# First mixer of a two-block transformer kernel: gate blocks between the heads, two softmaxes combined before the division, and GpSimd's wide steps given to other engines

## The chip, the cores and the metric

One core of a Trainium2 chip runs the whole program. The time is that of one execution on the device, in microseconds (us), as the median of three runs. Five engines work their own instruction lists in order and wait for each other by semaphores: TensorE (PE, matrix products), VectorE (DVE), ScalarE (ACT), GpSimd (POOL) and SyncE (SP, which here starts the weight transfers).

## The reference, cut to what matters

256 tokens of width 1024 pass through a feed-forward block, a mixer, a second feed-forward block, and then a second block of another kind, which the change doesn't touch. The mixer of the first block is:

```python
h = rmsnorm(x, g_pre_mix[l])
z = h @ w_in[l]
qa, ka, va, qd, kd, vd, ga, gb = jnp.split(z, cuts, axis=-1)
...
oa = diff_attention(qa, ka, va, lam)                 # 8 heads, two softmaxes each
oa = (rmsnorm(oa, g_subln[l]) * (1.0 - lambda_init)).reshape(B, S, DA_V_W)
...                                                  # 12 dilated heads in 3 groups: qd, kd, vd
od = jnp.sum(wts[..., None].astype(x.dtype) * jnp.stack(outs, axis=0), axis=0)
merged = jax.nn.sigmoid(ga) * (oa @ w_proj_a[l]) + jax.nn.sigmoid(gb) * (od @ w_proj_b[l])
x = x + rmsnorm(merged @ w_out[l], g_post_mix[l])
```

and inside `diff_attention`:

```python
s = jnp.einsum('bqhcd,bkhcd->bhcqk', qblk, k, preferred_element_type=jnp.float32) * scale
p = jax.nn.softmax(s, axis=-1)
a = p[:, :, 0] - lam * p[:, :, 1]
return jnp.einsum('bhqk,bkhe->bqhe', a.astype(v.dtype), v, ...)
```

## The kernel before, in words

All weights come as one stream of blocks of 128x1024 (512 KB), in the order in which `_stream` lists them. For each block ACT casts the raw weights to a rounded part wh (L243), and another engine subtracts it to get the rest, wl (L245): DVE, or POOL for every second block while `ws.pool_every` is 2. A product with such a block is three matmuls for each of its eight slices: wh with hT, wh with lT, wl with hT (L297 to L299), 24 matmuls for a column block of q, k or a gate. A block is split some blocks ahead of its use: each call of `ws.next()` puts one more cast and one more subtraction into the lists of ACT and DVE, at the place of the call.

The order of every engine's list is the order of the code. The work on attention is written as generators, which a pump holds; each `pump.step()` takes each active generator to its next `yield`, between two blocks of PE's products.

The first mixer runs in these stages. V of the heads (va). Then a loop over eight heads, two weight blocks each: q block, step, k block, step. A head (`diff_head`) takes several steps while the next heads' blocks are computed: rope (a shuffle on DVE, a product with ropeC on POOL, one with ropeS and a sum on DVE, giving qr), scores (PE into two banks acc), `exps` (a maximum and a scaled negative nb on DVE for each of the two score tiles, then two exponentials on ACT with row sums ls), the combination of the two softmaxes (ACT scales one by nb, DVE adds the other), four transposes (tr), a copy (aT), the product with va, and a copy of it into ov.

Then come the six dilated pairs of (s, g) in `MIX_ORDER`, two weight blocks each. After the third one, six blocks of V (vz) and the first gate blocks follow, and the other gate blocks after the sixth. Each dilated pair has its rope, its scores with a mask, its exponentials into the tile ed; after the third of a set, eight rounds of transposes, copies (eT) and products (od), then weights from the maxima (`weights`), a weighted sum over the groups (part), two transposes and a split (odH, odL). `subln` squares ov, sums it by head, takes the power -0.5 on POOL, multiplies ov, and transposes it into oaH and oaL. A list named `lock` sets which of the two sets and `subln` uses the transposes' banks. Last are the projection of oa (eight blocks), the merge with that of od, and w_out.

PSUM has eight banks here: two of tag mm (the blocks), three acc (scores), one od, two tr (transposes, products with va).

Of the kernel before, what the change touches and what calls it, by code (L numbers as in the profile page):

```python
# [50 lines left out]
# ---------------------------------------------------------------- layout on the host  # L51
# [22 lines left out]
GATES_A = 2  # L74
# [3 lines left out]
def _stream(a):  # L78
# [4 lines left out]
    qb, kb = _col_blocks(qa, 8, 1), _col_blocks(ka, 8, 1)  # L83
    for h in range(8):
# [3 lines left out]
    gab, gbb = _col_blocks(ga, 8, 1), _col_blocks(gb, 8, 1)  # L88
    gates = [w for c in range(8) for w in (gab[c], gbb[c])]
# [129 lines left out]
# ---------------------------------------------------------------- on the chip  # L219
# [57 lines left out]
def body(ctx, tc, a, o, upto=99):  # L277
# [17 lines left out]
    # matmul helpers on split operands  # L295
# [11 lines left out]
    def gemm_pair(outs, xs, shared=False):  # L307
        """Two products of the same operand, a block of it at a time; shared: outs lie in one bank."""
# [13 lines left out]
    def keep_busy(n, pt):  # L322
        """Keeps the tensor engine's clock up while it waits."""
# [15 lines left out]
    # ---- constants  # L339
# [31 lines left out]
    def inv_root(r, s, eps):  # L371
        """r = (s + eps) ** -0.5"""
# [4 lines left out]
    def row_sum(pool, src, p=128):  # L377
        """Mean squares of the rows."""
# [5 lines left out]
    def finish(acc, ops):  # L384
        """The last two steps of a token-major gemm, the first tile of tokens ahead of the second."""
# [5 lines left out]
    class RowNorm:  # L391
        """r = (mean square over factor ** 2 + eps over factor ** 2) ** -0.5 of 128 rows, by halves of the columns."""
# [17 lines left out]
    def close(pool, acc, g, factor, gi, tags, early=lambda n: None, fills=(), rest=20):  # L410
        """x += factor * rmsnorm(acc) * g, or x += acc, or x; hT, lT = the split of (rmsnorm(x) * g_pre) transposed."""
# [71 lines left out]
    def norm_meta(pool, gi):  # L483
        """hT, lT of the meta tokens."""
# [17 lines left out]
    # ---- feed-forward  # L502
# [47 lines left out]
    # ---- hyena filter in time; two thirds of its last product wait for turns of the tensor engine  # L550
# [55 lines left out]
    def mixer_tables(FP):  # L606
# [17 lines left out]
        # -lambda on all partitions  # L624
# [24 lines left out]
    # ---- mixer of the first block  # L649
    with tc.tile_pool(name="mix", bufs=1) as MP:  # L650
# [19 lines left out]
        def qk_block(qk, i):  # L670
            pt = psum("mm")
            gemm_w(pt[:, :T], ws.next(), xs_x)
            nc.scalar.copy(qk[:, i, :], pt[:, :T])
# [4 lines left out]
        def rope_pair(qk, res):  # L678
# [3 lines left out]
            nc.gpsimd.tensor_tensor(qk, qk, ropeC[:, None, :].to_broadcast([128, 2, T]), op=ALU.mult)  # L682
# [909 lines left out]
```

## Time and profile before

| | us |
|---|---|
| median of three runs | 1844.4 |
| lowest, highest of them | 1843.55, 1852.92 |
| span of the profiled execution (its own time lies around it) | 1849.8 |
| first mixer: V of the heads | from 209 to 232 |
| its loop over heads | from 232 to 345 |
| its dilated pairs, gates and projection | from 345 to 458 |
| its merge and w_out | from 458 to 495 |

The span counts from the first to the last instruction. PE's busy share of it is 95%, and the granted clock of PE over the whole span is 0.987 of full speed. An instruction that is busy on an engine off the path costs nothing by itself; what ends last is told by the chain of waits, and where PE stands by its timeline, in which a bracket tells how long it was idle before an instruction and which instruction released it.

### The profile page before, as it was taken

The page shows a single profiled execution, that of the slowest core. Times are in us where ns is not written, and L with a number is a line of the kernel's source. Part 1 is how long each engine was busy: PE and PEld are TensorE (multiplying, and loading weights), DVE is VectorE, ACT ScalarE, POOL GpSimd, SP SyncE. Part 2 cuts the span into 40 slices and gives each one's busy share as a digit, 9 for nine tenths or more (in the row PEclk, how much of TensorE's full clock was granted, in tenths as well). Part 3 has the DMA queues.
Part 4 walks back from the last instruction along what each step waited for, and adds up shares of the span by engine and source line. Part 5 has one row for each costly group of instructions (what it writes and reads, how often), then busy time and mean ns, then how long its engine had stood idle before and what let it go on. Part 6 is the DMA issues. An engine that isn't in the chain of part 4 may idle for free.

```text
span 1849.8 us, 30894 instructions
## 1 busy us (share of the span) xinstructions
PE 1750.3 (95%) x11794; PEld 1592.4 (86%) x11794; DVE 1343.0 (73%) x2040; ACT 927.6 (50%) x1495; POOL 725.8 (39%) x609
## 2 busy tenths in 40 slices
PE   8999998999999998899799899998999999999998
PEld 7999888999899977878789899998888888888886
DVE  5665678664655648985868998788888867777776
ACT  5544555554564435555445344454544445544554
POOL 3000133312200206444413354799999933322332
PEclk9999999999999999999999999999999999999999
DMA  7555543444565533433365457655555567767775
GB/s 237 190 176 186 162 145 104 149 129 160 183 205 196 180 135 120 146 105 100 115 193 185 146 196 234 206 178 176 178 176 163 170 233 256 244 227 234 250 242 173
DMA packets 93412, 332.09 MB, mean 180 GB/s; under 512 B 10552, under 2 KB 10707, under 8 KB 90960
## 3 DMA queue, kind: packets, MB, share of 16 engines
q1 hardware_dynamic: 79488, 287.73, 47.8%
q0 software_dynamic: 3696, 21.67, 3.4%
q10 hardware_dynamic: 10080, 20.71, 3.1%
q8 instruction: 93, 1.52, 0.3%
q14 instruction: 55, 0.45, 0.1%
HBM read 311.73 MB, written 18.35 MB: 178 GB/s over the span
## 4 chain that ended last, share of the span: by engine, by line
PE 59%; DVE 18%; POOL 12%; ACT 4%; issue 4%; DMA 3%; ACTq 0%; POOLq 0%; SPq 0%; DVEq 0%
PE mm L297 9%; PE mm L299 9%; PE mm L298 9%; POOL oh L1477 8%; PE acc L299 7%; PE acc L298 7%; PE acc L297 7%; DVE wl L245 5%; POOL wl L245 3%; PE od L297 2%; PE od L298 2%; PE od L299 2%; ACT wh L243 2%; DVE xc L1069 1%; DVE hu L1248 1%
## 5 line engine op out<-in xcount | busy, mean ns | idle before, releaser
L245 DVE TENSOR_TENSOR wl<-raw,wh 128x1024 fp32r<-128x1024 f32 x462 | 634.9, 1379 | 272.3 <-ACT wh L243 271.7
L297 PE MATMUL mm<-hT,wh 128*128 128x256 f32 (+1 forms) x2496 | 721.0, 289 | 8.0 <-DVE th L1281 4.7
L299 PE MATMUL mm<-hT,wl 128*128 128x256 f32 (+1 forms) x2496 | 709.0, 284 | 11.0 <-DVE wl L245 11.0
L298 PE MATMUL mm<-lT,wh 128*128 128x256 f32 (+1 forms) x2496 | 710.8, 285 | 0.0
L243 ACT CAST wh<-raw 128x1024 fp32r<-128x1024 f32 x544 | 568.3, 1049 | 271.4 <-PE mm L298 64.8
L297 PEld LDWEIGHTS mm<-hT,wh 128*128 128x128 f32 x2496 | 477.0, 191 | 18.1 <-issue 5.5
L299 PEld LDWEIGHTS mm<-hT,wl 128*128 128x128 f32 x2496 | 479.4, 192 | 12.2 <-DVE wl L245 12.2
L298 PEld LDWEIGHTS mm<-lT,wh 128*128 128x128 f32 x2496 | 477.2, 191 | 3.5 <-issue 1.4
L245 POOL TENSOR_TENSOR wl<-raw,wh 128x1024 fp32r<-128x1024 f32 x82 | 204.0, 2488 | 233.0 <-ACT wh L243 186.7
L1477 POOL TENSOR_SCALAR oh<-iota,eT 128x128 fp32r<-128x128 f32 x256 | 233.8, 930 | 11.3 <-PE acc L1488 11.3
L299 PE MATMUL acc<-wh,al 128*128 128x512 f32 x516 | 202.1, 392 | 0.7 <-DVE al L337 0.7
L298 PE MATMUL acc<-wl,ah 128*128 128x512 f32 x516 | 202.0, 391 | 0.5 <-DVE wl L245 0.4
L297 PE MATMUL acc<-wh,ah 128*128 128x512 f32 x516 | 202.1, 392 | 0.0
L1478 DVE SCALAR_TENSOR_TENSOR oh<-iota,eT,wp 128x256 fp32r<-128x256 f32 x256 | 147.4, 610 | 0.1
L403 POOL TENSOR_SCALAR ssq<-ssq 128x1 f32<-128x1 f32 x18 | 8.5, 471 | 299.0 <-ACT junk L401 270.0
L299 PEld LDWEIGHTS acc<-wh,al 128*128 128x128 f32 x516 | 96.9, 188 | 22.9 <-DVE al L337 1.7
L298 PEld LDWEIGHTS acc<-wl,ah 128*128 128x128 f32 x516 | 96.8, 188 | 20.9 <-DVE wl L245 1.6
L297 PEld LDWEIGHTS acc<-wh,ah 128*128 128x128 f32 x516 | 96.9, 188 | 19.3 <-issue 0.3
L336 ACT CAST ah<-sv 128x256 fp32r<-128x256 f32 x124 | 50.2, 405 | 111.4 <-PE od L298 43.0
L1520 POOL TENSOR_TENSOR sv<-sv,gd 128x512 f32<-128x512 f32 x62 | 96.1, 1580 | 6.1 <-DMA sv<-act 5.8
L337 DVE TENSOR_TENSOR al<-sv,ah 128x256 fp32r<-128x256 f32 x124 | 72.3, 583 | 33.4 <-ACT ah L336 33.4
L1512 POOL DMA_DIRECT2D sv<-act x16 | 9.6, 599 | 213.2 <-DVE al L337 209.2
(388 smaller groups left out, 2334.9 us busy)
## 6 DMA issues: line engine op xcount, KB each, us to landing
raw<-in_ws_dram SPq DMA_DIRECT2D x288, 512.0 KB, 3.7
raw<-in_us_dram SPq DMA_DIRECT2D x128, 512.0 KB, 3.7
raw<-in_vs_dram SPq DMA_DIRECT2D x128, 512.0 KB, 4.3
act<-st ACTq DMA_DIRECT2D x62, 256.0 KB, 3.0
sv<-act POOLq DMA_DIRECT2D x15, 1024.0 KB, 7.8
gate_w<-in_gate_w_dram ACTq DMA_DIRECT2D x2, 1024.0 KB, 7.0
gain<-in_gains_dram POOLq DMA_DIRECT2D x3, 512.0 KB, 6.4
res<-x SPq DMA_DIRECT2D x2, 512.0 KB, 4.5
```

Source lines behind the costliest of these rows:

```text
L243: nc.scalar.copy(h, raw)
L245: eng.tensor_tensor(lo, raw, h.bitcast(F32), op=ALU.subtract)
L297: nc.tensor.matmul(out, lh, rh, start=start, stop=False)
L298: nc.tensor.matmul(out, lh, rl, start=False, stop=False)
L299: nc.tensor.matmul(out, ll, rh, start=False, stop=stop)
L336: nc.scalar.copy(h, src)
L337: (eng or nc.vector).tensor_tensor(lo, src, h.bitcast(F32), op=ALU.subtract)
L1069: nc.vector.scalar_tensor_tensor(out, src, w, out, op0=ALU.mult, op1=ALU.add)
L1248: nc.vector.scalar_tensor_tensor(out, t[:, j:j + L], w, out, op0=ALU.mult, op1=ALU.add)
L1477: nc.gpsimd.tensor_scalar(o1, iota, eT[tt][:, 0, tl:tl + 1], None, op0=ALU.is_equal)
L1478: nc.vector.scalar_tensor_tensor(oh, iota[:, None, :].to_broadcast([128, 2, 128]), eT[tt][:, 1, tl:tl + 1], wp[:, :, tl:tl + 1].bitcast(F3 ...
L1520: nc.gpsimd.tensor_tensor(src, src, gd[:, e:e + 2, :], op=ALU.mult)
```

## The change

It concerns the first mixer alone. The stream of weights now has a gate block behind each head's q and k, and the other eight gate blocks together behind the dilated pairs. The scale of the scores goes into ACT's copy of q, so the maxima need no product: `exps` takes a maximum with its sign turned. The two softmaxes of a head are combined as e0 + r1 * e1 with r1 = -lam * l0 / l1, and the division by l0 is left to ACT, as the scale of the copy of the product with va. POOL's product with ropeC goes to DVE, behind the shuffle, with a `yield` less. POOL's weight subtractions go to DVE (`pool_every` stays 0). `subln` is added after the first dilated pair instead of the third, squares on ACT and multiplies on DVE, and has its transposes before the first set's od; the sums of part and of the merge go from POOL to DVE. The two small operations of the power -0.5 stay on POOL. Comments go, by which line numbers shift.

```diff
     for h in range(8):
-        units += [qb[h], kb[h]]
+        units += [qb[h], kb[h], gab[h]]
...
         if n == 2:
-            units += list(vb) + gates[:2 * GATES_A]
-    units += gates[2 * GATES_A:]
+            units += list(vb)
+    units += list(gbb)
...
+            if i:
+                nc.scalar.copy(qk[:, i, :], pt[:, :T])
+            else:
+                nc.scalar.activation(qk[:, i, :], pt[:, :T], AF.Copy, scale=DA_SCALE)
...
             nc.vector.stream_shuffle(sw, qk, SWAP)
-            nc.gpsimd.tensor_tensor(qk, qk, ropeC[:, None, :].to_broadcast([128, 2, T]), op=ALU.mult)
-            yield
+            nc.vector.tensor_tensor(qk, qk, ropeC[:, None, :].to_broadcast([128, 2, T]), op=ALU.mult)
...
-                nc.vector.tensor_reduce(mx[:, :, c], sc[c], axis=AX.X, op=ALU.max)
-                nc.vector.tensor_scalar(nb[:, :, c], mx[:, :, c], -DA_SCALE, None, op0=ALU.mult)
+                nc.vector.tensor_reduce(nm[:, :, c], sc[c], axis=AX.X, op=ALU.max, negate=True)
...
-            nc.vector.reciprocal(ls, ls)
-            nc.vector.tensor_scalar(nb[:, :, 1], ls[:, :, 1], nlam, None, op0=ALU.mult)
+            nc.vector.reciprocal(r1, ls[:, :, 1])
+            nc.vector.scalar_tensor_tensor(r1, r1, nlam, ls[:, :, 0], op0=ALU.mult, op1=ALU.mult)
             for qt in range(2):
-                nc.scalar.activation(e[:, qt, 1, :], e[:, qt, 1, :], AF.Copy, scale=nb[:, qt, 1:2])
-                nc.vector.scalar_tensor_tensor(e[:, qt, 0, :], e[:, qt, 0, :], ls[:, qt, 0:1],
-                                               e[:, qt, 1, :], op0=ALU.mult, op1=ALU.add)
+                nc.vector.scalar_tensor_tensor(e[:, qt, 0, :], e[:, qt, 1, :], r1[:, qt:qt + 1], e[:, qt, 0, :],
+                                               op0=ALU.mult, op1=ALU.add)
+            nc.vector.reciprocal(ls[:, :, 0], ls[:, :, 0])
...
-            nc.vector.tensor_copy(ov[:, :, h, :], pv[:, :T].rearrange("p (q e) -> p q e", q=2))
+            for qt in range(2):
+                nc.scalar.activation(ov[:, qt, h, :], pv[:, qt * 128:qt * 128 + 128], AF.Copy, scale=ls[:, qt, 0:1])
...
-                nc.gpsimd.tensor_tensor(sq[sl], ov[sl], ov[sl], op=ALU.mult)
+                nc.scalar.activation(sq[sl], ov[sl], AF.Square)
...
-                nc.gpsimd.tensor_tensor(ov[sl], ov[sl], ss[sl][:, :, None].to_broadcast([128, 4, 128]), op=ALU.mult)
+                nc.vector.tensor_tensor(ov[sl], ov[sl], ss[sl][:, :, None].to_broadcast([128, 4, 128]), op=ALU.mult)
...
-        ws.pool_every = 2
+        def gate_block(i, c):
+            pt = psum("mm")
+            gemm_w(pt[:, :T], ws.next(), xs_x)
+            nc.scalar.copy(sg[i][:, c, :], pt[:, :T])
+            pump.step()
...
             pump.add(diff_head(h, qk))
             pump.step()
+            gate_block(0, h)
...
-            while s and lock[:1] != [2]:
+            while lock[:1] != [0 if s else 2]:
...
-            nc.gpsimd.tensor_tensor(pa, pa, part[:, 1], op=ALU.add)
-            nc.gpsimd.tensor_tensor(pa, pa, part[:, 2], op=ALU.add)
+            nc.vector.tensor_tensor(pa, pa, part[:, 1], op=ALU.add)
+            nc.vector.tensor_tensor(pa, pa, part[:, 2], op=ALU.add)
...
             pump.step()
+            if n == 0:
+                pump.add(subln())
             if n == 2:
-                pump.add(subln())
...
-        gate_blocks(GATES_A, 8)
+        while lock[:1] != [2] and lock[:1] != [0]:
+            pump.step()
+        sg.append(MP.tile([128, 8, T], F32, tag="va", name="sg_b"))
+        for c in range(8):
+            gate_block(1, c)
+            pump.step()
...
-        ws.pool_every = 2
         for c in range(8):
...
             pump.step()
+            pump.step()
         pump.drain()
-        ws.pool_every = 0
...
-            nc.gpsimd.tensor_tensor(m, m, sg[0][:, c:c + 2, :], op=ALU.add)
+            nc.vector.tensor_tensor(m, m, sg[0][:, c:c + 2, :], op=ALU.add)
```

DVE's list for one lap of the loop over heads, before; e is the tile of exponentials, mx, nb and ls its maxima, biases and row sums, sw and qr the tiles of rope:

```order
L245 TENSOR_TENSOR wl<-raw,wh 128x1024
L749 COPY ov<-tr 128x2x128
L731 RECIPROCAL ls<-ls 128x4
L732 TENSOR_SCALAR nb<-ls,nlam 128x2
L735 SCALAR_TENSOR_TENSOR e<-e,ls 128x256 x2
L681 STREAM_SHUFFLE sw<-qk 128x512
L705 TENSOR_REDUCE mx<-acc 128x2
L706 TENSOR_SCALAR nb<-mx 128x2
L705 TENSOR_REDUCE mx<-acc 128x2
L706 TENSOR_SCALAR nb<-mx 128x2
L684 TENSOR_TENSOR sw<-sw,ropeS 128x512
L686 TENSOR_TENSOR qr<-qk,sw 128x512
```

The same lap now; nm are the maxima with their sign turned, r_3064 is r1:

```order
L243 TENSOR_TENSOR wl<-raw,wh 128x1024 x2
L706 TENSOR_REDUCE nm<-acc 128x2 x2
L243 TENSOR_TENSOR wl<-raw,wh 128x1024
L732 RECIPROCAL r_3064<-ls 128x2
L733 SCALAR_TENSOR_TENSOR r_3064<-r_3064,nlam,ls 128x2
L735 SCALAR_TENSOR_TENSOR e<-e,r_3064 128x256 x2
L737 RECIPROCAL ls<-ls 128x2
L682 STREAM_SHUFFLE sw<-qk 128x512
L683 TENSOR_TENSOR qk<-qk,ropeC 128x512
L684 TENSOR_TENSOR sw<-sw,ropeS 128x512
L686 TENSOR_TENSOR qr<-qk,sw 128x512
```

Rope stood in two parts, around the next maxima; now it is one piece behind the sums in e, and three subtractions of weights stand in the lap instead of one.

ACT's list for such a lap, before; wh is the cast of a weight block, qk the copy of a q or k block:

```order
L243 CAST wh<-raw 128x1024
L673 COPY qk<-mm 128x256
L708 ACTIVATE e,ls<-acc,nb 128x256 x4
L243 CAST wh<-raw 128x1024
L673 COPY qk<-mm 128x256
L741 COPY aT<-tr 128x512
L734 ACTIVATE e<-e,nb 128x256 x2
```

And now; L674 is the copy of q with the scale, L672 that of k, sg_a the gate:

```order
L674 ACTIVATE qk<-mm 128x256
L751 ACTIVATE ov<-tr,ls 128x128 x2
L241 CAST wh<-raw 128x1024
L672 COPY qk<-mm 128x256
L742 COPY aT<-tr 128x512
L708 ACTIVATE e,ls<-acc,nm 128x256 x4
L241 CAST wh<-raw 128x1024
L797 COPY sg_a<-mm 128x256
L241 CAST wh<-raw 128x1024
```

The four exponentials stood behind the copy of a q block; now they stand behind those of a k block and of aT, and a cast stands between them and the copy of the gate.

DVE's list around the norm of the heads, now (mxd are the maxima of a dilated pair, sq and ss squares and sums of `subln`):

```order
L706 TENSOR_REDUCE mxd<-acc 128x2 x2
L243 TENSOR_TENSOR wl<-raw,wh 128x1024
L765 TENSOR_REDUCE ss<-sq 128x4 x4
L682 STREAM_SHUFFLE sw<-qk 128x512
L683 TENSOR_TENSOR qk<-qk,ropeC 128x512
L684 TENSOR_TENSOR sw<-sw,ropeS 128x512
L686 TENSOR_TENSOR qr<-qk,sw 128x512
L243 TENSOR_TENSOR wl<-raw,wh 128x1024
L773 TENSOR_TENSOR ov<-ov,ss 128x512 x4
L706 TENSOR_REDUCE mxd<-acc 128x2 x2
```

Before, POOL's list had the squares and the products of ov at that step, all four of each in one piece:

```order
L682 TENSOR_TENSOR qk<-qk,ropeC 128x512 x4
L763 TENSOR_TENSOR sq<-ov 128x512 x4
L768 TENSOR_SCALAR ss<-ss 128x16
L769 TENSOR_TENSOR ss<-ss,nhalf 128x16
L773 TENSOR_TENSOR ov<-ov,ss 128x512 x4
```

The four products with ov moved from POOL into DVE's list, ahead of the next pair's maxima.

## Rows read from the trace of the kernel before

**Rows 1.** The page, first part: busy time, share of the span, instructions.
```profile
span 1849.8 us, 30894 instructions
PE 1750.3 (95%) x11794; PEld 1592.4 (86%) x11794; DVE 1343.0 (73%) x2040; ACT 927.6 (50%) x1495; POOL 725.8 (39%) x609
```

**Rows 2.** Windows: stretch, us, busy PE, PEld, DVE, ACT, POOL, clock, DMA, GB/s.
```profile
232.00:345.00 113.00, 102.63 (x829) 94.93 (x828) 90.48 (x145) 65.73 (x158) 39.82 (x23) 1.00 0.37 123
345.00:459.00 114.00, 113.89 (x956) 111.15 (x954) 64.14 (x103) 58.43 (x103) 25.30 (x17) 1.00 0.46 149
```

**Rows 3.** Chain that ended last, 200 to 520: start us, us, what.
```profile
282.55 0.94 ACT wh L243
...
289.69 1.75 DVE nb L706
...
292.48 0.94 ACT wh L243
```

**Rows 4.** PE's timeline, 290.9 to 293.2: start, us, instruction, [idle before <- releaser].
```profile
292.86 0.70 PE L699 MATMUL acc<-qr 64*128 64x256 f32 x4 [1.58 <-DVE qr L686]
```

**Rows 5.** Chain that ended last, 246 to 258.
```profile
246.79 1.06 PE acc L699 x8
247.85 0.32 PE mm L297
...
250.93 0.38 ACT qk L673
```

**Rows 6.** ACT's timeline, 318 to 345 and 352 to 378.
```profile
319.08 0.47 ACT L708 ACTIVATE e<-acc,nb 128x256 f32<-128x256 f32 x1 [2.29 <-DVE nb L706]
...
320.90 1.06 ACT L243 CAST wh<-raw 128x1024 fp32r<-128x1024 f32 x1
...
355.84 0.59 ACT L859 COPY eT<-tr 128x512 f32<-128x512 f32 x1
356.32 1.06 ACT L243 CAST wh<-raw 128x1024 fp32r<-128x1024 f32 x1
```

**Rows 7.** DVE's timeline, 318 to 345.
```profile
319.75 0.68 DVE L684 TENSOR_TENSOR sw<-sw,ropeS 128x512 f32<-128x512 f32 x1
320.54 0.69 DVE L686 TENSOR_TENSOR qr<-qk,sw 128x512 f32<-128x512 f32 x1
321.98 1.23 DVE L245 TENSOR_TENSOR wl<-raw,wh 128x1024 fp32r<-128x1024 f32 x1 [0.75 <-ACT wh L243]
323.12 0.42 DVE L749 COPY ov<-tr 128x256 f32<-128x256 f32 x1
323.46 0.17 DVE L731 RECIPROCAL ls<-ls 128x4 f32<-128x4 f32 x1
323.66 0.23 DVE L732 TENSOR_SCALAR nb<-ls,nlam 128x2 f32<-128x2 f32 x1
324.52 0.89 DVE L735 SCALAR_TENSOR_TENSOR e<-e,ls 128x256 f32<-128x256 f32 x2 [0.64 <-ACT e L734]
...
325.33 0.74 DVE L681 STREAM_SHUFFLE sw<-qk 128x512 f32<-128x512 f32 x1
```

**Rows 8.** POOL's timeline, 325 to 368.
```profile
333.57 1.27 POOL L682 TENSOR_TENSOR qk<-qk,ropeC 128x512 f32<-128x512 f32 x1 [5.24 <-DVE sw L681]
...
355.30 1.11 POOL L768 TENSOR_SCALAR ss<-ss 128x16 f32<-128x16 f32 x1 [12.39 <-DVE ss L765]
356.49 2.92 POOL L769 TENSOR_TENSOR ss<-ss,nhalf 128x16 f32<-128x16 f32 x1
```

**Rows 9.** Chain that ended last, 352 to 364.
```profile
359.25 0.84 PE od L868 x8
```

**Rows 10.** PE's timeline, 748 to 751, in the second block.
```profile
750.53 0.79 PE L1091 MATMUL acc<-xc,gate_w 128*128 128x272 f32 x1 [2.42 <-DVE xc L1069]
```

**Rows 11.** Windows around that wait.
```profile
745.00:750.00 5.00, 3.11 (x25) 2.89 (x23) 4.82 (x9) 2.37 (x6) 0.51 (x1) 1.00 0.29 81
750.00:755.00 5.00, 4.47 (x19) 4.04 (x20) 4.86 (x7) 1.20 (x2) 2.38 (x1) 0.66 0.32 129
```

More of the change, by code (lines that the diff above doesn't have):

```diff
@@ L83, in _stream @@
     qb, kb = _col_blocks(qa, 8, 1), _col_blocks(ka, 8, 1)
+    gab, gbb = _col_blocks(ga, 8, 1), _col_blocks(gb, 8, 1)
     for h in range(8):
-        units += [qb[h], kb[h]]
+        units += [qb[h], kb[h], gab[h]]
     qb, kb = _col_blocks(qd, 8, 1), _col_blocks(kd, 8, 1)
     vb = vd.reshape(2, 4, 128, 3, 256).transpose(3, 0, 2, 1, 4).reshape(6, 128, 1024)
-    gab, gbb = _col_blocks(ga, 8, 1), _col_blocks(gb, 8, 1)
-    gates = [w for c in range(8) for w in (gab[c], gbb[c])]
     for n, (s, g) in enumerate(MIX_ORDER):
@@ L701, in scores, with exps @@
             return [sc.rearrange("p (q t) -> p q t", q=2) for sc in out]
[L703 removed]
+        def exps(sc, e, nm, ls):
             for c in range(2):
[L705 to L706 removed]
+                nc.vector.tensor_reduce(nm[:, :, c], sc[c], axis=AX.X, op=ALU.max, negate=True)
                 for qt in range(2):
[L708 to L709 removed]
+                    nc.scalar.activation(e[:, qt, c, :], sc[c][:, qt, :], AF.Exp, bias=nm[:, qt, c:c + 1],
+                                         accum_out=ls[:, qt, c:c + 1])
         def transpose4(src):
@@ L758, in subln @@
                 yield
-            sq = MP.tile([128, 2, 8, 128], F32, tag="big", name="sq", bufs=1)
+            sq = MP.tile([128, 2, 8, 128], F32, tag="va", name="sq")
             ss = MP.tile([128, 2, 8], F32, name="ss")
-            for c in range(4):
-                sl = (slice(None), c // 2, slice(4 * (c % 2), 4 * (c % 2) + 4))
-                nc.gpsimd.tensor_tensor(sq[sl], ov[sl], ov[sl], op=ALU.mult)
-                yield
+            parts = [(slice(None), c // 2, slice(4 * (c % 2), 4 * (c % 2) + 4)) for c in range(4)]
+            for sl in parts:
+                nc.scalar.activation(sq[sl], ov[sl], AF.Square)
                 nc.vector.tensor_reduce(ss[sl], sq[sl], axis=AX.X, op=ALU.add)
+            squares.append(True)
             sv = ss.rearrange("p q h -> p (q h)")
@@ L830, in dil_scores @@
                          MP.tile([128, 3, 2, 2], F32, tag="mxd", name="mxd", bufs=2),
-                         MP.tile([128, 3, 2, 2], F32, tag="nbd", name="nbd", bufs=2),
                          MP.tile([128, 3, 2, 2], F32, tag="lsd", name="lsd", bufs=2))
-            e, mx, nb, ls = dl[s]
-            exps(sc, e[:, g], mx[:, g], nb[:, g], ls[:, g])
+            e, mx, ls = dl[s]
+            exps(sc, e[:, g], mx[:, g], ls[:, g])
             if g < 2:
@@ L885, in dil_scores @@
             split(odH[:, s, :], odL[:, s, :], pt[:, :T])
-        sg = []
-        def gate_blocks(c0, c1):
-            if not sg:
-                sg.extend(MP.tile([128, 8, T], F32, tag=t, name=f"sg_{t}") for t in ("va", "big"))
-            for c in range(c0, c1):
-                for i in range(2):
-                    pt = psum("mm")
-                    gemm_w(pt[:, :T], ws.next(), xs_x)
-                    if i:
-                        nc.scalar.copy(sg[i][:, c, :], pt[:, :T])
-                    else:
-                        nc.vector.tensor_copy(sg[i][:, c, :], pt[:, :T])
-                    pump.step()
         for n, (s, g) in enumerate(MIX_ORDER):
@@ L936, in body @@
             pump.step()
+            pump.step()
         pump.drain()
-        ws.pool_every = 0
         merged = []
```

58 lines of the change are left out of this document (26 added, 32 removed).

## The prediction

> **What bounds the kernel now.** I read the page first, then the two halves of the first mixer in the view by windows, then the chain of waits there, then each engine's timeline for one lap of the head loop. The page says that TensorE (PE) is busy for 1750.3 us of 1849.8 [rows 1], so an edit pays only where PE waits. The windows bound the gain at once: PE is busy for 102.63 of 113 us in the first half of the mixer (the heads) and for 113.89 of 114 in the second, both at a granted clock of 1.00 [rows 2]. That leaves 10.4 + 0.1 = 10.5 us of idle PE in all that the change touches. It adds and removes no matmuls. However well it works, it can win about 10.5 us, 0.57% of 1844.4.
>
> Where these 10.4 us lie, the chain shows: one lap of a head lasts 292.48 - 282.55 = 9.93 us, and runs through DVE and ACT [rows 3]. Once a lap PE stands before the scores, for 1.58 us, until DVE has made qr [rows 4]. PE's own work in a lap is thus 9.93 - 1.58 = 8.35 us. A typical piece of that chain is a 128x2 product (nb, L706) that lasts 1.75 us [rows 3].
>
> **What a lap is made of afterwards.** The order shows three weight blocks in a lap instead of two. PE takes 2.9 us for a block of 24 matmuls: the first starts at 247.85, ACT's copy at 250.93, of which the last matmul's drain is some 0.2 [rows 5]. So PE needs 8.35 + 2.9 = 11.25 us. If nothing else were late, all idle time would be gone.
>
> DVE loses nb (twice a lap), the copy of ov and its wait for POOL's product; it gains the product with ropeC and two more weight subtractions of 1.14 [rows 7]. The sum of its lap is 3 x 1.14 (wl) + 0.8 (shuffle) + 3 x 0.7 (rope) + 2 x 0.7 (maxima, priced as a product of that size) + 0.8 (e) + 0.5 (small) = 9.0 us, of 11.25: no engine is full. But each engine works its list in order, and I follow the order round. From one head's scores to the next head's scores it passes through everything once:
>
> - PE: scores to the next k block, 247.85 - 246.79 = 1.06; that block to ACT's copy of k, 250.93 - 247.85 = 3.08 [rows 5]. ACT reaches the exponentials only behind this copy.
> - ACT: copy of k, 0.28 (0.38 less the overlap of 0.1 with the next instruction); copy of aT, 356.32 - 355.84 = 0.48; four exponentials, 320.90 - 319.08 = 1.82; then the cast of the next weights, 1.08 until DVE starts on them (321.98) [rows 6, 7].
> - DVE: wl, 1.14 (323.12 - 321.98); reciprocal and small product, which wait for each other, 2 x 0.20 (323.66 - 323.46); the two sums in e, 325.33 - 324.52 = 0.81; the second reciprocal 0.1 [rows 7].
> - DVE, behind that in its list, the next head's rope: shuffle 0.85 (the product with ropeC overwrites what it reads and so waits for its end: 0.74 and 0.11, the gap between sw's end and qr), product with ropeC 0.60, with ropeS 0.79, qr 0.69, and 0.05 to PE [rows 7].
>
> The product with ropeC does not stand on DVE in this trace. Its bounds are 0 (if it lay wholly under its neighbours) and the 1.27 that POOL took (L682) [rows 8]; I take 0.60, a 128x512 product of 0.68 (L684) less 0.08 of overlap. Together 1.06 + 3.08 + 0.28 + 0.48 + 1.82 + 1.08 + 1.14 + 0.40 + 0.81 + 0.10 + 0.85 + 0.60 + 0.79 + 0.69 + 0.05 = 13.23 us a lap. PE needs 11.25, so it stands for 2.0 us a lap before the scores: more than the 1.58 now. The weight work of the new block pays for itself on no engine's total, but one cast and one subtraction of it stand in the ring, and the rope stands behind the sums in e instead of ahead of them. The first lap has no aT and no product with va: 12.75 against 10.3, 2.4 us. Sum of the heads: 2.4 + 6 x 2.0 = **14.4 us** (between 9 and 19, with 1.2 to 2.7 a lap).
>
> **The norm of the heads (subln).** It now stands ahead of the V blocks' second half, and PE's transposes of ov are in front of the third dilated scores. I count from the end of the last head's scores. The wl behind exps(7) is done at 7.9. DVE then goes on without a pause: e and small 1.3, rope 2.85, two wl 2.3, rope 2.85, wl 1.1, first maximum 0.7, so 19.0. ACT, which waited for it, does four exponentials 1.8, a cast 0.95, two scalings of ov at 0.27 each, four squares; these were POOL's and are on ACT for the first time, bounded by 0.48 (a copy of the same size) and 1.06 (a cast of twice the size), and I take 0.5 [rows 6]. With the last row sum of 0.7 it is 25.1. Then POOL's two small operations, which the change leaves there: 1.11 + 2.92 with 0.1 between [rows 8], 29.3. DVE's products with ov are three of 0.65 until PE may start: 31.3. PE has by then 8 blocks (23.2), two products with va, four transposes and two scores to do, 28.4. It waits 2.9 us. The next scores need a bank of acc that exps(1) of the dilated part frees, whose maximum stands on DVE behind all four products: 1.6 more. Sum **4.5 us** (2 to 6).
>
> **The dilated part.** The rest overlaps more tightly than before: six exponential groups, the second half of them while the first half's products still run. exps of (1,0) overwrite the tile ed and wait for the last transpose of (0,2); behind them on ACT stand a cast, a copy of a gate and the eT that PE wants: 1.8 + 0.95 + 0.3 + 0.6 = 3.7 us after that transpose, when PE has 2.3 of other work (a product od of 0.84, masks and scores [rows 9]): 1.4 us. The same kind of queue gives about 1.7 at the last scores, 2.0 at the second transpose of (1,2), 0.7 at the last transpose of ov: 5.8 by such sums. PE comes a little later to each than its plain sum says, so I take **4.0** (1 to 6).
>
> **The clock.** In this stage 1.58 us of standing left the clock at 1.00 [rows 2, 4]. Further on, PE stood for 2.42 us before an acc, and the stretch behind had a granted clock of 0.66, between its two levels of 1.2 and 2.4 GHz: 5 x 0.34 = 1.7 us lost [rows 10, 11]. One wait of mine, the 2.9 at the norm, is longer, so I add **1.7**. The Trainium skill (TensorE: Matmul & The Clock Gate, section "Why this matters for your kernels") tells the kernel writer to leave no long idle gaps between bursts of matmuls, as the engine drops to its lower level; the trace agrees in the stretch with 0.66. What that does if the 2.0 us of each lap are enough is a rival below.
>
> **What I cost at nothing.** The gate copies go to ACT, 0.4 each, which PE's 11.25 us of a lap cover. The scale in the copy of q and the maximum with its sign turned take the place of operations of the same size. The merge's sums on DVE take POOL's place where PE has 5 us of other products; without that cover they would cost 4 x 0.7. The weight split of the projection goes to DVE, which has room there (64 of 114 us busy in the second half). The last odH no longer stands right before its reader: a gain of at most 0.5, left out.
>
> **Sum.** New waits 14.4 + 4.5 + 4.0 + 1.7 = 24.6; old ones gone, 10.5. The change makes the kernel 14.1 us slower. The profiled execution has a span of 1849.8, which lies 5.4 above the median of the runs and below the slowest (1852.92). The sum is a difference, so I set it on the median: 1844.4 + 14.1 = **1858.5 us**.
>
> **Rivals.**
> - *The heads become bound by PE, and the kernel is faster.* For it speaks that nb is slow only beside POOL: 1.75 us where a dependent small product takes 0.20 [rows 3, 7]. The Trainium skill says why (GPSIMD Engine Reference, section 1, Specifications): GpSimd shares its SBUF interface with VectorE. By that rule DVE's list shortens by about 2 us, and this change would be the cure; the trace agrees that the product is slow, and only that. Against it: nb is not in my ring, and the ring has PE's block and four engines' waits in it. It decides if a lap's ring is below 11.25. Time: 1844.4 - 10.5 + 1 = 1835.
> - *About even.* The ring is at its lower end (12.4, 1.2 a lap, 8.6 in the heads), the norm costs 2 and the rest 1: +1, 1845.5. It decides if the product with ropeC and the wl lie under other work, or ACT passes the copy of k early.
> - *The clock falls in each lap.* 7 x 1.7 = 12 more: 1870. For it: the wait grows from 1.58 to 2.0, and 2.42 was enough elsewhere. Against it: there PE had been less busy before, 3.11 of 5 us, as the window view has it; here it works over 11 us in each lap.
>
> **Chances.** The forecast 0.63, PE-bound heads 0.05, even 0.24, the clock 0.08. The likeliest one's own range is 1851 to 1866. For 8 in 10, I go below to the even case with its norm and rest at nothing (1844.4 + 8.6 - 10.5 = 1842.5), and above to the clock's case: 1842 to 1870. About 0.5% (9.2 us) is what a measurement of this kernel can tell from no change. Slower by more: most of the forecast (0.54) and the clock's case, with a little of the even one, 0.64. Within 0.5%: 0.32. Faster by more would need nearly all of the 10.5 us: 0.04.
>
> **What would show it.** Right: in the heads PE waits about 2 us a lap before the scores, the releaser is DVE's qr, and a lap lasts 13.2 us; the chain there runs k block, ACT's copy, exponentials, cast, wl, e, rope. nb is gone, and POOL is idle in the mixer but for the two small operations. PE waits at the first transpose of ov for DVE's product, some 3 us. In the second half of the mixer PE idles for some 10 us where now it is 0.1. Wrong: laps of 11.3 us with no wait at the scores; the exponentials starting ahead of the copy of k; or a PE that is as busy in the second half as before.

## The result, and the profile after

The changed kernel takes 1867.18 us (median of 4 runs, 1863.53 to 1870.88), the kernel before 1843.97 in the same session (4 runs, 1842.13 to 1852.92). The ratio on record for these runs is 1.0107 with an interval of 1.0084 to 1.0129: about 20 us slower (the medians alone differ by 23.2), where 14.1 were forecast. Below, "the stretch" is the time in a trace from the first q block of the mixer to the first transposes behind w_out. It took 259.1 us before (232.37 to 491.51) and takes 280.1 after (232.25 to 512.32), 20.9 more. What lies outside it took 1590.7 us before and from 1585.5 to 1595.6 in the profiled executions of the other versions below, though no edit touches it, so the stretch is the sharper measure of an edit here. Each stretch is that of one profiled execution.

The first part of the page after, which answers to [rows 1]:

```profile
span 1868.8 us, 30803 instructions
PE 1758.6 (94%) x11790; PEld 1602.6 (86%) x11794; DVE 1337.6 (72%) x2042; ACT 929.0 (50%) x1507; POOL 661.5 (35%) x567
```

POOL has lost 64 us of work. No wait of PE between the first q block and w_out had ended on POOL before. The windows after, for [rows 2] (columns as there):

```profile
232.00:345.00 113.00, 98.72 (x773) 92.59 (x772) 71.25 (x119) 54.49 (x130) 0.00 (x0) 0.95 0.39 127
345.00:459.00 114.00, 106.09 (x853) 99.59 (x856) 66.36 (x108) 61.26 (x133) 3.73 (x3) 0.97 0.36 116
```

Before, PE was busy for 102.63 and 113.89 us in the first two. Now it idles in both, and the granted clock is below 1.00 in both, where it was 1.00. DVE is busy for 71 of these 113 us, where it was for 90: no engine is full, and yet PE waits.

PE's timeline shows where it stands in a lap. Two successive laps, to be read with [rows 4]:

```profile
299.08 0.70 PE L699 MATMUL acc<-qr 64*128 64x256 f32 x4 [1.99 <-DVE qr L686]
...
312.28 0.49 PE L699 MATMUL acc<-qr 64*128 64x256 f32 x2 [1.99 <-DVE qr L686]
```

A lap is 312.28 - 299.08 = 13.20 us, and PE stands for 1.99 of it; the forecast had 13.23 and 2.0. The chain of waits through that lap, to be read with [rows 3, 5]:

```profile
299.08 1.14 PE acc L699 x8
300.22 0.32 PE mm L295
...
303.29 0.06 ACT qk L672
...
303.56 0.59 ACT aT L742
304.15 1.83 ACT e L708 x8
305.99 0.94 ACT wh L241
...
306.95 1.22 DVE wl L243
308.17 0.09 DVE r L732
...
308.28 0.23 DVE r L733
...
308.54 0.88 DVE e L735 x2
309.42 0.01 DVE ls L737
309.44 0.74 DVE sw L682
...
310.20 0.69 DVE qk L683
310.90 0.61 DVE sw L684
...
311.53 0.70 DVE qr L686
...
312.28 1.13 PE acc L699 x8
```

It runs as the prediction's ring does (the path from one head's scores through ACT and DVE to the next head's): scores, k block, copy of k, copy of aT, exponentials, cast, wl, the small operations and sums in e, rope, scores. The single links are up to 0.16 us longer or shorter than forecast (aT 0.59 for 0.48, the product with ropeS 0.63 for 0.79), and these differences cancel.

At the norm of the heads and the dilated scores next to it, PE's timeline has three waits, 3.58 us in all:

```profile
371.15 0.33 PE L782 MATMUL tr<-ident,ov 128*128 128x128 f32 x1 [1.22 <-DVE ov L773]
372.36 0.55 PE L782 MATMUL tr<-ident,ov 128*128 128x128 f32 x3 [0.87 <-DVE ov L773]
...
374.61 0.59 PE L694 MATMUL acc<-masks,identb 128*128 128x512 bf16 x1 [1.49 <-ACT ed L708]
```

And there is one that the prediction did not have, at the third block of the projection; first PE's row, then ACT's and DVE's timelines ahead of it:

```profile
462.12 0.39 PE L295 MATMUL mm<-oaH,wh 128*128 128x256 f32 x1 [2.05 <-DVE sg_a L931]
```

```profile
454.53 1.28 ACT L924 ACT_TABLE_LOAD   x1
455.82 1.92 ACT L924 ACTIVATE sg_a<-sg_a 128x2048 f32<-128x2048 f32 x1
457.64 1.90 ACT L925 ACTIVATE sg_b<-sg_b 128x2048 f32<-128x2048 f32 x1
459.44 1.03 ACT L241 CAST wh<-raw 128x1024 fp32r<-128x1024 f32 x1
```

```profile
460.51 1.23 DVE L243 TENSOR_TENSOR wl<-raw,wh 128x1024 fp32r<-128x1024 f32 x1 [7.14 <-ACT wh L241]
461.65 0.42 DVE L931 TENSOR_TENSOR sg_a<-mm,sg_a 128x256 f32<-128x256 f32 x1
```

PE needs a bank that DVE's product L931 frees. That product was ready to run when sg_a's sigmoid ended (457.7), but in DVE's list it stands behind a wl, whose cast stands behind the second sigmoid on ACT.

The clock is read from the windows:

```profile
256.00:262.00 6.00, 5.57 (x33) 4.87 (x34) 3.85 (x5) 0.00 (x0) 0.00 (x0) 0.72 0.52 164
283.00:289.00 6.00, 4.65 (x25) 3.83 (x26) 4.73 (x6) 0.79 (x1) 0.00 (x0) 0.72 0.39 119
337.00:343.00 6.00, 4.32 (x22) 3.50 (x23) 5.06 (x7) 1.12 (x2) 0.00 (x0) 0.72 0.37 122
373.00:379.00 6.00, 4.51 (x18) 3.15 (x18) 3.18 (x4) 4.88 (x12) 0.00 (x0) 0.50 0.29 110
```

It fell at the first, third and seventh wait in the heads and at the waits of the norm. A mean of 0.72 over 6 us is a part at 0.5, which is the lower level, and the rest at the upper. A lap with a fall lasts 14.7 us instead of 13.2, so a fall costs 1.5 us. Before the change PE once waited as long, ahead of the third head's scores, and the clock stayed at 1.00 (PE's row, and the window around it):

```profile
263.11 1.13 PE L699 MATMUL acc<-qr 64*128 64x256 f32 x8 [1.99 <-DVE qr L686]
```

```profile
256.00:270.00 14.00, 12.01 (x102) 11.42 (x101) 12.13 (x21) 8.67 (x22) 5.68 (x4) 1.00 0.34 115
```

The stretch closes by this account (windows 232 to 491 before, 232 to 512 after). PE's idle time in it was 10.55 us and is 24.24: 13.7 more. Its busy time rose from 248.45 to 255.76 us with the same matmuls: 7.3 more, which is put down to the clock. 13.7 + 7.3 = 21.0, of 20.9.

### The profile page after: what moved, and what is told of

Same layout as the page of the kernel before. It is cut to its first block, busy times and chain, and to the rows that moved or that the text cites. A ratio compares the mean times of both kernels' runs of the same rounds, so it can differ in the third digit from the quotient of the medians.

```text
span 1868.8 us, 30803 instructions
## 1 busy us (share of the span) xinstructions
PE 1758.6 (94%) x11790; PEld 1602.6 (86%) x11794; DVE 1337.6 (72%) x2042; ACT 929.0 (50%) x1507; POOL 661.5 (35%) x567
## 4 chain that ended last, share of the span: by engine, by line
PE 59%; DVE 17%; POOL 11%; ACT 6%; issue 4%; DMA 3%; ACTq 0%; POOLq 0%; SPq 0%; DVEq 0%
PE mm L295 9%; PE mm L297 9%; PE mm L296 9%; POOL oh L1473 7%; PE acc L297 7%; PE acc L295 7%; PE acc L296 7%; DVE wl L243 4%; POOL wl L243 3%; ACT wh L241 2%; PE od L295 2%; PE od L296 2%; PE od L297 2%; DVE xc L1065 2%; DMA raw<-in_us_dram 1%
## 5 line engine op out<-in xcount | busy, mean ns | idle before, releaser
L297 PE MATMUL mm<-hT,wl 128*128 128x256 f32 (+1 forms) x2496 | 712.5, 285 | 11.1 <-DVE wl L243 11.1
L1473 POOL TENSOR_SCALAR oh<-iota,eT 128x128 fp32r<-128x128 f32 x256 | 228.1, 907 | 16.1 <-PE acc L1484 16.1
L243 POOL TENSOR_TENSOR wl<-raw,wh 128x1024 fp32r<-128x1024 f32 x70 | 178.3, 2548 | 151.3 <-ACT wh L241 146.7
L1474 DVE SCALAR_TENSOR_TENSOR oh<-iota,eT,wp 128x256 fp32r<-128x256 f32 x256 | 151.5, 626 | 0.1
L335 DVE TENSOR_TENSOR al<-sv,ah 128x256 fp32r<-128x256 f32 x124 | 77.7, 626 | 42.0 <-ACT ah L334 42.0
L1516 POOL TENSOR_TENSOR sv<-sv,gd 128x512 f32<-128x512 f32 x62 | 101.6, 1666 | 6.0 <-DMA sv<-act 5.7
L1489 ACT COPY gd<-acc 128x256 f32<-128x256 f32 x128 | 47.2, 400 | 78.9 <-PE acc L1484 64.1
```

Source lines behind the costliest of these rows:

```text
L243: eng.tensor_tensor(lo, raw, h.bitcast(F32), op=ALU.subtract)
L297: nc.tensor.matmul(out, ll, rh, start=False, stop=stop)
L335: (eng or nc.vector).tensor_tensor(lo, src, h.bitcast(F32), op=ALU.subtract)
L1473: nc.gpsimd.tensor_scalar(o1, iota, eT[tt][:, 0, tl:tl + 1], None, op0=ALU.is_equal)
L1474: nc.vector.scalar_tensor_tensor(oh, iota[:, None, :].to_broadcast([128, 2, 128]), eT[tt][:, 1, tl:tl + 1], wp[:, :, tl:tl + 1].bitcast(F3 ...
L1489: nc.scalar.copy(g, v[:, 1])
```

## The experiments

Each is the changed kernel with the edit shown. Ratios are to the kernel before, measured beside it on the same chip; the changed kernel's is 1.0107. The times named in the expectations count from the 1867 us of the changed kernel above; the kernel before had medians of 1848.36 to 1852.1 us beside the other runs, so ratios and stretches are what can be compared.

| edit | stretch, us | lap, us | ratio (interval) |
|---|---|---|---|
| before | 259.1 | 9.9 | 1 |
| the change | 280.1 | 13.2 | 1.0107 (1.0084 to 1.0129) |
| exponentials with the scores | 261.3 | 11.25 | 1.0011 (0.9987 to 1.0035) |
| youngest head first | 271.3 | 12.26 | 1.0106 (1.0087 to 1.0125) |
| gate blocks behind | 279.1 | 11.1 | 1.0127 (1.0110 to 1.0144) |
| 14 fillers (matmuls of the identity) | 284.9 | 14.27 | 1.0143 (1.0126 to 1.0160) |
| 8 fillers | 279.4 | 13.26 | 1.0116 (1.0089 to 1.0142) |
| POOL's share in the projection | 280.7 | 13.2 | 1.0127 (1.0095 to 1.0160) |
| second sigmoid late | 278.4 | 13.2 | 1.0100 (1.0065 to 1.0135) |
| norm's transposes behind | 280.6 | 13.2 | 1.0124 (1.0097 to 1.0151) |
| norm's products behind too | 278.8 | 13.2 | 1.0092 (1.0058 to 1.0126) |
| three edits, first set | 266.1 | 11.24 | 1.0040 (1.0023 to 1.0057) |
| three edits, second set | 259.2 | 11.23 | 0.9973 (0.9956 to 0.9991) |
| with the norm spread out | 256.2 | 11.23 | 0.9962 (0.9945 to 0.9980) |

### Is the lap a ring?

**Exponentials with the scores.**

```diff
             sc = scores(res[0], None)
-            yield
             e = MP.tile([128, 2, 2, T], F32, tag="e", name="e", bufs=2)
```

> One yield less in a head: its exponentials are listed in the same step as its scores, so ACT reaches them behind the copy of the next q and not behind that of the next k, and the sums in e come a step earlier. Ring theory (the lap is as long as the ring scores, k block, copy of k, exponentials, cast, wl, sums in e, rope): the ring loses the k block and its copy (3.4 us) and falls to 10.9, under PE's 11.25. Laps of 11.3 to 11.5 us, waits before the scores 0.3 us at most, granted clock in the heads 1.00. Time 1867 - 14 (waits) - 5 (clock) = 1848, within 1844 to 1853. Rival, DVE or ACT as a whole is too slow for three weight blocks a lap: laps stay near 13, PE waits 1.5 us or more, time 1862 or more.

Laps of 11.25 us, and between two of them PE's timeline shows no wait before the scores (the first lap alone has one, 0.63 us):

```profile
266.67 1.13 PE L699 MATMUL acc<-qr 64*128 64x256 f32 x8
...
277.91 1.14 PE L699 MATMUL acc<-qr 64*128 64x256 f32 x8
```

The window of the heads:

```profile
232.00:345.00 113.00, 111.98 (x917) 106.28 (x916) 84.72 (x141) 66.01 (x160) 0.00 (x0) 1.00 0.47 148
```

PE is busy for 111.98 of 113 us at a clock of 1.00. The stretch loses 18.8 us, where 19 were expected. All three weight blocks, with all their casts and subtractions, fit into 11.25 us: the rival with a full engine is out, and the kernel is level with the one before. Not all of it was won: the two waits for ov at the norm grew from 2.09 to 4.37 us.

**Youngest head first.**

```diff
+    newest_first = False
...
-        for g in list(self.active):
+        for g in list(self.active)[::-1 if self.newest_first else 1]:
...
+        pump.newest_first = True
         for h in range(8):
...
             gate_block(0, h)
+        pump.newest_first = False
```

> In the loop over heads each step takes the youngest head first, so the next head's rope stands ahead of the sums in e in DVE's list, and nothing else changes. Ring theory: the ring loses the sums and the small operations (1.3 us) and is 11.9; laps of 11.9 us, PE waits 0.6 to 0.7 us before the scores, and with so short a wait the clock stays at 1.00. Time 1867 - 9 (waits) - 5 (clock) = 1853, within 1849 to 1859. Rival, rope isn't what the scores wait for last: laps stay at 13.2 and the time at 1867.

```profile
279.87 1.13 PE L701 MATMUL acc<-qr 64*128 64x256 f32 x8 [0.93 <-DVE qr L688]
...
292.13 1.13 PE L701 MATMUL acc<-qr 64*128 64x256 f32 x8 [0.92 <-DVE qr L688]
```

PE's timeline has a wait of 0.92 us and a lap of 12.26, of which 11.9 was forecast: shorter by 0.94, not by 1.3. The direction is the ring's. The stretch lost 8.7 us, 14 were expected; a wait of 1.87 us at the transposes of the last head's e, with a fall of the clock, is new. The runs did not show the gain (1.0106): in the profiled execution the rest of the kernel, which the edit does not touch, took 1595.6 us, some 7 more than with the change. Why is open.

**Gate blocks behind the dilated pairs.**

```diff
-        units += [qb[h], kb[h], gab[h]]
+        units += [qb[h], kb[h]]
...
-    units += list(gbb)
+    units += list(gab) + list(gbb)
...
-            gate_block(0, h)
+            pump.step()
...
+        for c in range(8):
+            gate_block(0, c)
         while lock[:1] != [2] and lock[:1] != [0]:
```

> The gate blocks go from the loop over heads to behind the dilated pairs, and the third step of a lap stays. Ring theory: the ring loses one cast and one wl (2.2 us) and is 11.0, while PE has 8.35 us of work; laps of 11.0 us with waits of 2.7 us, so the block isn't what makes PE wait, it fills 2.9 us and lengthens the ring by 2.2. Time 1867 - 7 x 2.2 + 8 x 2.9 = 1875, within 1870 to 1884 with the clock. Rival, the weight work of the gate block is what makes the lap long: laps of 8.4 to 8.7 us without a wait, time about 1852.

```profile
286.89 1.14 PE L699 MATMUL acc<-qr 64*128 64x256 f32 x8 [1.57 <-DVE qr L686]
...
292.02 1.16 PE L747 MATMUL tr<-va,aT 128*128 128x128 f32 x8 [0.95 <-ACT aT L742]
...
298.01 1.13 PE L699 MATMUL acc<-qr 64*128 64x256 f32 x8 [1.55 <-DVE qr L686]
```

Laps of 11.1 us with 2.5 us of waiting (11.0 and 2.7 forecast), not 8.4. So the gate block is not what makes PE wait. Without it a lap is 2.1 us shorter and has 2.9 us less of useful work. The time did not come out as expected: the stretch is 1.0 us shorter, not 8 longer, because the heads ended 20 us earlier (the first lap and the clock gained too) and the gate blocks, now behind, covered most waits of the dilated part.

### Is it the clock?

```diff
             out = [psum("acc") for _ in range(2)]
+            if mask is None:
+                keep_busy(14, out[0])
```

> 14 matmuls of 128x128 of the identity, into the bank that the scores then overwrite, stand in PE's list ahead of each head's scores and fill some 1.5 us of the wait there. Clock theory (three of the seven waits of 2 us in the heads brought the clock down, some 5 us lost): laps stay at 13.2 us, the granted clock in the heads is 1.00 in every window, and the time is 1867 - 5 = 1862, within 1859 to 1865. Rival, the clock falls for another reason, or the 1.5 us delay the scores: 1867 or more.

> As the run with 14 matmuls of the identity ahead of each head's scores, but with 8, which by that run take 0.214 us each, 1.7 us in all, and so end within the wait of 2.0 us. Clock theory: laps stay at 13.2 us, PE waits 0.3 us before the scores, the granted clock in the heads is 1.00 in every window, and the stretch from the first q block to the transposes behind w_out falls from 280.1 to 275 us (273 to 277). Rival, the clock falls for another reason: 280, with falls in the heads.

The second has 8 in place of 14. The 14 took 3.0 us, not 1.5, more than the wait of 2.0, so PE never stood before the scores and laps were 14.27: the first run is the rival's case of fillers that delay. Its clock in the window of the heads was 1.00 too. With 8 the fillers end within the wait. PE's timeline and the window of the heads:

```profile
298.50 1.20 PE L701 MATMUL acc<-qr 64*128 64x256 f32 x8 [0.19 <-DVE qr L686]
...
311.76 1.20 PE L701 MATMUL acc<-qr 64*128 64x256 f32 x8 [0.20 <-DVE qr L686]
```

```profile
232.00:345.00 113.00, 111.27 (x919) 106.87 (x919) 71.80 (x120) 56.53 (x138) 0.00 (x0) 1.00 0.41 129
```

All laps behind the first last 13.26 us, none 14.7, at a clock of 1.00. So it is the standing of PE that brings the clock down here, though not at every wait. The gain fell short: of 4.5 us (three falls of 1.5) the fillers ahead of the first head's scores, where PE hardly waits, took back 1.8, and the clock fell once at the projection, where it had not with the change. The stretch lost 0.7, not 5, and the runs show no gain.

### The wait in the projection

Two edits, each alone: POOL's share as before the change, and the second sigmoid later.

```diff
+        ws.pool_every = 2
         for c in range(8):
             pt = psum("mm")
             gemm_w(pt[:, :T], ws.next(), oxs)
...
         pump.drain()
+        ws.pool_every = 0
```

```diff
-        nc.scalar.activation(sg[1], sg[1], AF.Sigmoid)
...
             nc.vector.tensor_tensor(sg[0][:, c, :], pt[:, :T], sg[0][:, c, :], op=ALU.mult)
+            if c == 2:
+                nc.scalar.activation(sg[1], sg[1], AF.Sigmoid)
```

> Every second weight subtraction of the projection goes back to POOL, and nothing else. Theory: the wait of 2.05 us at the third projection block (DVE's product with the gate stands behind a subtraction whose cast waits for both sigmoids on ACT) goes or falls under 0.8, and the stretch from the first q block to the transposes behind w_out falls from 280.1 to 278 us (277 to 279.5). Rival, the two sigmoids and casts on ACT alone hold it: the wait stays near 2 us, 280 or more.

> The changed kernel with one edit: the second gate's sigmoid stands behind the third projection block in ACT's list. Theory: the wait of 2.05 us at the third projection block falls under 0.4, all else stays, and the stretch from the first q block to the transposes behind w_out falls from 280.1 to 278 us (277 to 279.5, if the clock falls as often as there). Rival, the first sigmoid and its table load (3.2 us) hold it just as well: the wait stays over 1.5.

PE's rows at the third block, with POOL's share (first fence) and with the late sigmoid:

```profile
461.52 0.39 PE L295 MATMUL mm<-oaH,wh 128*128 128x256 f32 x1 [2.05 <-DVE sg_a L932]
```

```profile
460.39 0.39 PE L295 MATMUL mm<-oaH,wh 128*128 128x256 f32 x1 [0.25 <-DVE sg_a L930]
```

POOL's share does nothing: my theory of that run fell, its rival held. The second sigmoid's place is the cause, 2.05 to 0.25, and the stretch falls by 1.7 us to 278.4, where 278 was expected.

### The norm of the heads

First its transposes go back behind the first dilated set, as before the change:

```diff
             for sl in parts:
                 nc.vector.tensor_tensor(ov[sl], ov[sl], ...)
             yield
+            while lock[:1] != [0]:
+                yield
             pts = {}
...
-            while lock[:1] != [0 if s else 2]:
+            while s and lock[:1] != [2]:
```

Then its products too, and the loop of bare steps ahead of the gate blocks ends earlier:

```diff
+            while lock[:1] != [0]:
+                yield
             for sl in parts:
                 nc.vector.tensor_tensor(ov[sl], ov[sl], ...)
...
-            while lock[:1] != [0 if s else 2]:
+            while s and lock[:1] != [2]:
...
-        while lock[:1] != [2] and lock[:1] != [0]:
+        while not squares:
```

> The transposes of the norm of the heads go back behind the first dilated set, as before the change; its squares and products stay where they are. Theory: PE no longer waits for the products of ov (1.22 + 0.87 us), and the fall of the clock behind it (some 3 us) goes or shrinks; the wait before the masks (1.5 us), which hangs on the maxima behind these products, stays. The stretch from the first q block to the transposes behind w_out falls from 280.1 to 275 us (273 to 278). Rival, what was late is only moved: new waits of 2 us or more in the second dilated set, 279 to 282.

> The norm's products with ov go behind the first dilated set in DVE's list, with its transposes, and the second set's steps follow the blocks without bare steps between them; the heads stay as they are. Theory (the products, which wait for POOL's power, hold up the maxima of the second dilated pair that stand behind them): the wait before the masks, 4.46 us where only the transposes went back, falls under 0.5, no wait for ov is over 0.5, and the clock stays at 1.00 there. The heads keep laps of 13.2 us. The stretch from the first q block to the transposes behind w_out falls from 280.1 to 273 us (271 to 276). Rival, the wait at the masks comes from elsewhere: it stays at 4 us, and the stretch at 278 to 281.

PE's rows at the masks, with the transposes alone moved (first fence) and with the products too:

```profile
374.90 0.59 PE L694 MATMUL acc<-masks,identb 128*128 128x512 bf16 x1 [4.46 <-ACT ed L708]
```

```profile
372.15 0.38 PE L694 MATMUL acc<-masks,identb 128*128 128x512 bf16 x1 [2.04 <-ACT ed L708]
```

Moving the transposes only carried the wait on: 3.58 us in three places became 4.46 in one, and the stretch stayed (280.6). That is in the rival's range. With the products away as well it fell to 2.04, not under 0.5, so the products were part of what held up the masks. New waits of 1.8 and 0.9 us came at ov, whose products then stood right ahead of its transposes; a third of 1.4, which hangs on oaL, was there already with the transposes alone moved. The clock stayed at 1.00 at the masks and fell at ov instead, and once more at the projection. The rest of that theory did not hold: the stretch, 278.8 and not 273, is in the range that the rival gave.

### Versions made of these

The first joins three of the edits above, word for word: the exponentials, POOL's share and the transposes.

> Three edits together: exponentials in the step of the scores, POOL's share of the projection's subtractions, the norm's transposes behind the first dilated set. From the run with the exponentials alone (261.3 us for the stretch from the first q block to the transposes behind w_out) the wait of 2.04 at the projection, 4.37 at the transposes of ov and some 2.8 of slow clock behind it go: 252 us (250 to 257), against 259.1 before the change: 7 us or 0.4% faster than before. Rival, the waits come back elsewhere: 259 or more, no faster than before.

The stretch was 266.1 us, not 252, and the kernel 0.4% slower than before: the rival's case. The wait at the masks grew to 7.73 us: with faster heads PE comes to it 18.1 us earlier than where the transposes alone were moved, and it ends only 14.9 us earlier. The chain behind it is in DVE's timeline: the products wait for POOL's power, and the next pair's rope, a wl and the maxima stand behind them.

```profile
351.99 2.50 DVE L772 TENSOR_TENSOR ov<-ov,ss 128x512 f32<-128x512 f32 x4 [3.09 <-POOL ss L769]
...
358.24 1.28 DVE L706 TENSOR_REDUCE mxd<-acc 128x2 f32<-128x512 f32 x2
```

The next joins the exponentials, the products behind the first set and the late sigmoid:

> The edit of the products together with two more: the exponentials in the step of the scores, and the second gate's sigmoid behind the third projection block in ACT's list instead of ahead of all of its casts. Theory: laps of 11.3 us, no wait at the masks or for ov over 0.5, and at the third projection block 0.4 us or less instead of 2.04, since that wait is ACT's second sigmoid (1.9 us) ahead of a cast that DVE's list waits for. The stretch from the first q block to the transposes behind w_out is 254 us (250 to 258), against 259.1 before the change and 261.3 with the exponentials alone: 5 us or 0.3% faster than before. Rival, the projection's wait isn't the sigmoid or the second dilated set waits more: 259 or more.

By the runs it is 0.3% faster than before, 0.9973 (0.9956 to 0.9991); its profiled execution, the slowest of its 12, has a stretch of 259.2, outside the 250 to 258 expected and no shorter than before, so the trace doesn't show where the gain lies. The projection's wait is gone, that at the masks is 2.16. Last, beside the early exponentials and the late sigmoid, the norm's squares, sums and products go one at a time into successive steps (the edit's lines on `squares`, the second set's lock, the exponentials and the sigmoid are as above):

```diff
                 nc.scalar.activation(sq[sl], ov[sl], AF.Square)
+                yield
                 nc.vector.tensor_reduce(ss[sl], sq[sl], axis=AX.X, op=ALU.add)
...
             nc.gpsimd.tensor_tensor(sv, sv, nhalf, op=ALU.pow)
             yield
+            yield
             for sl in parts:
                 nc.vector.tensor_tensor(ov[sl], ov[sl], ...)
-            yield
+                yield
+            while lock[:1] != [0]:
+                yield
```

> As the run with the three edits (exponentials early, products of ov behind the first set, second sigmoid late), but the squares, sums and products of the heads' norm go one at a time into successive steps, the products ahead of the first set's last step. Theory: the four sums in one piece (2.5 us) were what held up the maxima ahead of the masks, and the four products in one piece what the transposes of ov waited for; the waits of 2.16 at the masks and of 1.77, 0.87 and 1.40 at ov fall under 0.5 each, and the clock's fall behind the first goes. The stretch from the first q block to the transposes behind w_out falls from 259.2 to 252 us (250 to 255); 7 us or 0.4% faster than before the change. Rival, the waits hang on the order of the second set itself: 257 or more.

```profile
354.16 0.38 PE L694 MATMUL acc<-masks,identb 128*128 128x512 bf16 x1 [1.79 <-ACT ed L708]
...
410.19 0.66 PE L785 MATMUL tr<-ident,ov 128*128 128x128 f32 x4 [1.64 <-DVE oaL L790]
```

The stretch is 256.2 us, between the theory's range and the rival's: the waits at ov fell from 4.0 to 1.9 us (1.64 of what is left hangs on oaL, not on the products), that at the masks only from 2.16 to 1.79, so the four sums in one piece were not its main cause, which stays open. At 0.9962 (0.9945 to 0.9980) it has the lowest ratio of these, though its interval overlaps that of the version ahead of it: all of the change's parts but their order, and faster than the kernel before. How much of that the edits made is open: the ratio stands for some 7 us, the medians (1843.56 against 1848.36) differ by 4.8, and the stretch is 2.9 us shorter; the rest was traced to no edit.

## Why the prediction was right, and where its sum was off

The time lies within the stated 1842 to 1870, but just above the forecast's own 1851 to 1866 and nearer to the rival with the clock (1870).

*The bound.* No engine's total work kept the 10.5 us from being won: the run with early exponentials has PE busy for 111.98 of 113 us in the heads. The change put longer waits in place of the old ones, as the sum has it.

*The heads, 14.4.* Measured 2.34 + 1.98 + 5 x 1.99 = 14.3 us, with the releaser, the lap and the chain as forecast. The run with the early exponentials shows that the list order made it: one `yield` less leaves 0.6 us of it. The run without gate blocks bears out the sentence that the block's cast and subtraction stand in the ring.

*The norm, 4.5.* 3.6 measured. The chain was partly another: POOL's two operations were no later than DVE's own list (the products had a wl in front, with no idle time between). Only in two versions with faster heads (early exponentials alone, and the first three edits) did POOL's power come last.

*The dilated part, 4.0.* 4.1 measured (five waits of 0.3 to 1.4, and two small ones).

*The clock, 1.7.* This is the mis-sized term: 7.3 measured. The prediction had one fall, behind the norm, and gave the falls in each lap a chance of 0.08. Three of the seven waits in the heads brought one, 4.5 us, and the norm's, with several waits behind each other, cost some 2.8, which is what is left of the 7.3. The rival was half true, and its argument against itself (PE works for over 11 us in each lap) did not hold. Nor does the wait's growth from 1.58 to 2.0 us explain the falls by itself: the wait of 1.99 us ahead of the third head's scores before the change, which the prediction did not use, brought none.

*What was costed at nothing.* The projection was, and it cost 2.05 us. I had looked at DVE's room there, which it has, and not at what stands ahead of each subtraction on ACT. Before, the second set's products still stood between the first projection blocks (its last od at 448.36, the projection from 429.02), and after they end ahead of it (451.2 and 453.9). That this cover is all that is missing is not borne out: in the run with the norm's products moved, which leaves both sigmoids in place, some of these products stand between the projection blocks again, and ahead of the third block PE waits for a copy (eT) that stands behind the same sigmoids:

```profile
455.87 1.76 PE L877 MATMUL acc<-vz,eT 128*128 128x64 f32 x8 [1.68 <-ACT eT L868]
```

*GpSimd.* The rival that DVE without POOL beside it would win the heads had its cause right and its weight wrong. Before, nb took 1.72 us at 250.20 and so ended at 251.92, where POOL's wl ended (251.90), and 0.17 us at 331.77 and 332.57, where POOL had no work beside it. But nb was not in the new ring: it is gone, DVE has less to do, and the laps grew.

Sum: 14.3 + 3.6 + 4.1 + 2.05 + 0.2 = 24.2 of waits, 7.3 of clock, less 10.5: 21.0, against 14.1. Of the 6.9 missing, 5.6 are the clock.

## What to carry to other kernels

When engines work lists in order, follow the path once round a lap from an instruction to itself and sum it: here a lap was the longer of that ring and the fullest engine (13.2 us by the ring, 11.25 by PE once the ring was shorter), and neither busy shares nor the amount of moved work told which. When a block is added, ask at which place of the ring its preparation stands; one step earlier for the exponentials, which everybody waits for, took back 18.8 of the 20.9 us that the whole change cost. Price a wait on PE that recurs with the clock that it may cost, and look at what stands behind a long single instruction on an otherwise idle engine.

## What the runs showed of the hardware

Waits of the same length did not all bring the clock down: of the seven in the heads, three did here, behind the first, third and seventh; in other runs with the same heads it was the first and fourth, the first, fourth and seventh, or the first, third and sixth. At the projection the wait of 2.04 to 2.27 us, there in nine of the profiled executions, brought a fall in two (8 fillers, POOL's share: windows of 0.79 over 8 us) and none in seven (1.00). Waits of 0.92 in the heads with the youngest first, and of 1.99 and 1.58 before the change [rows 2, 4], brought none there. A fall in the heads cost 1.5 us a lap (laps of 14.7 against 13.2).

The length of a tiny operation on POOL went with what DVE did beside it: the same scaling of 128x16 took 1.11 us before [rows 8] and 1.16 in the first run with three edits, where DVE was in a wl, and 0.20 after, where it was in a shuffle. The two long ones ended 0.1 us behind the end of that wl (356.41 and 356.34; 348.96 and 348.90), though they began 0.1 to 0.2 us behind its start. The power behind it took 2.92, 2.91 and 2.91.
